# Stick-breaking attention in a hybrid block: the scan's zero operand in PSUM, 513-wide scans from two sigmoid tiles, two query buffers

## The chip, the cores and the metric

The kernel runs on one core of a Trainium2 chip. TensorE (PE) multiplies into PSUM, VectorE (DVE), ScalarE (ACT) and GpSimd (POOL) do the elementwise work, and SyncE (SP) issues the DMAs. The metric is the device time of one execution in microseconds.

## The reference

One layer over 2048 tokens of 1024 features: a modulated norm, one input projection, two groups of heads, an output projection with residual, a second modulated norm, and a convolutional feed-forward part. The change lies in the stick-breaking attention of eight heads of 64:

```python
def stick_breaking_attention(q, k, v):
    """A[t,s] = beta_ts * prod_{s<j<t}(1-beta_tj), s<t, in log space."""
    ...
        z = jnp.einsum('bhqd,bhkd->bhqk', qb, kb).astype(jnp.float32) * scale
        mask = s_pos[None, :] < t_pos[:, None]
        log_one_minus = jnp.where(mask, jax.nn.log_sigmoid(-z), 0.0)
        shifted = jnp.concatenate(
            [log_one_minus[..., 1:], jnp.zeros_like(log_one_minus[..., :1])], axis=-1)
        between = lax.cumsum(shifted, axis=3, reverse=True)
        weights = jnp.where(mask, jnp.exp(jax.nn.log_sigmoid(z) + between), 0.0)
        outs.append(jnp.einsum('bhqk,bhkd->bhqd', weights.astype(vb.dtype), vb))
```

Per query the weight of a key is its sigmoid times the product of (1 - sigmoid) over all later keys, so a running product from the last key back to the first is wanted.

## The kernel before

The program has three parts: the input projection with the gated linear attention (to about 663 us in the profile), the stick-breaking attention with the output projection running alongside (to about 1400 us), and the feed-forward part. The attention works on units (j, h, ci): 512 queries of chunk j, head h, 512 keys of chunk ci, from ci = j (the diagonal one) down to 0. Four chunks and eight heads give 80 units; each has four steps of 128 queries, so there are 320 steps n: 32 in the first chunk of queries, 64, 96 and 128 in the following ones. Half of the second chunk's steps, a third of the third's and a quarter of the fourth's are diagonal ones, which are 128, 256, 384 and 512 keys wide; all others are 512 wide.

Step n issues in this order: `score(n)`, two products of queries (high and low parts) and keys into a PSUM tile z of two buffers, and on the diagonal a product with a mask; `weigh(n-1)`; `turned(n-6)`, the transposes of the weights into a PSUM tile tr; `value(n-8)`, two products with the values into av. In `weigh`, ACT writes om = sigmoid(-z/8) and bt = sigmoid(z/8); DVE scans om in place from the last column to the first (a running product: multiply by the element, add zero), and POOL multiplies bt by om shifted by one column. Column 512 of om holds what the running product was at the end of the next later keys' unit: a copy of column 0 of the om of four steps before, which is also the scan's start value. In `turned`, ACT copies tr to ah and DVE subtracts, al = tr - ah. PE's order in the loop is that of the program (`in_order`); the order on the other engines is set by a planner that simulates the program.

PSUM has eight banks. In the first chunk of queries they hold z (2), tr (2), av (2) and the sums of the last input projection; `swap_pools` then gives tr a third bank (`t2`, every third turn) and the output projection one. `project` puts the output projection of chunk j among the steps of chunk j+1 as 64 groups of three products, at a rate that spreads them over the chunk; after the first chunk it starts 24 steps late. `fetch` loads, six steps ahead, keys (kt), values (vt) and, for a new head, queries (qh, ql; pool `qp`, three buffers). In the fourth chunk POOL also makes sums for the feed-forward part (`early_sums`, tiles tq).

Of the kernel before, what the change touches and what calls it, by code (L numbers as in the profile page):

```python
# [16 lines left out]
P = 128  # L17
# [3 lines left out]
CH = 512  # L21
# [26 lines left out]
def hybrid_block(ctx, tc, x, c, w_ada, b_ada, g1, w_in, w_fg2, b_fg2, g_gla, w_out, g2,  # L48
# [24 lines left out]
    def in_order(engines=None):  # L73
        """what the block traces is issued, on each engine, in the order of the program"""
# [57 lines left out]
    # ================= in-projection and gated linear attention =================  # L132
# [15 lines left out]
    # small parameters, rows of 128 turned into columns  # L148
# [20 lines left out]
    def ada_sum(m, acc):  # L169
        """products of silu(c) and the rows of w_ada, still to be summed over the partitions"""  # L170
# [14 lines left out]
    def column_sums(acc):  # L185
        """the sums over the partitions of 1024 columns, as columns"""
        tp = ps_tp.tile([P, CH], F, name="tp")
        for k in range(KD):
            pe.matmul(out=tp[:, k:k + 1], lhsT=acc[:, k * P:(k + 1) * P], rhs=ones[:, 0:1], start=True, stop=True)
        return tp[:, :KD]  # L190

    # scale and shift before the in-projection, as columns
# [4 lines left out]
    def ada_load(ks, buf, off, cuts):  # L197
        """the columns of w_ada for the shift and scale of some of the features"""
# [8 lines left out]
    def ada_columns(ks, w, name):  # L207
        """their products with silu(c), as columns"""
# [37 lines left out]
    # columns of the convolution's parameters  # L246
# [10 lines left out]
    # strict suffix sums within chunks of 64, and the chunks' indicators  # L257
# [32 lines left out]
    def w_block(c0):  # L290
        """128 columns: [k][hi, lo] as (128 rows, 128 columns)"""
# [7 lines left out]
    def w_rows(c0, n):  # L299
        """n columns, all rows: [k][hi, lo]"""  # L300
# [14 lines left out]
    def load_gla(k0, n, pl, s=None):  # L315
        """rows of the weights of GLA's queries and keys"""
# [6 lines left out]
    def split_gla(k0, n, s, w=None, lo=None):  # L323
        """their parts, with the forget gate's first product behind the keys: by k, [hi, lo]"""
# [12 lines left out]
    def gla_parts(ws):  # L337
        """the weights of 128 queries, again, and of the keys and the forget gate: [k][hi, lo]"""
# [7 lines left out]
    def norm_x(j, tt):  # L346
        """128 rows of x over their norm"""
# [16 lines left out]
    def turn_x(j, k):  # L364
        """128 of the features for the whole chunk: turned, modulated, and split"""
# [39 lines left out]
    # A tile of 128 tokens (two chunks of the recurrence) is laid out with a head's parity and a token of a chunk on the  # L405
    # partitions, and with the chunk, the pair of heads and the features along them; queries and keys are zero outside of
    # their own head, so that a product over a pair of heads has no columns to spare.
# [12 lines left out]
    def gla_tile(ti):  # L420
        """a tile of 128 tokens, in stages"""
# [54 lines left out]
    def by_parity(t_):  # L476
        """columns (pair of heads, head, n) taken as (head, pair of heads, n)"""
        return t_.rearrange("p (a b n) -> p b a n", a=2, b=2)
# [26 lines left out]
    def gla_inputs(j, wq, wk, begun=None):  # L505
        """GLA's queries, keys and log decays of a chunk; the sums may have been made"""
# [22 lines left out]
        # log of the forget gate (times 16): min(z, 0) - ln(1 + exp(-|z|))  # L529
# [19 lines left out]
        # the chunks' whole decays  # L549
# [11 lines left out]
    def gla_rows(j, w, gated):  # L561
        """GLA's values, or its output gate, of a chunk"""
# [12 lines left out]
    def heads_qk(j, w, b):  # L575
        """128 of the attention's queries (b < 4) or keys of a chunk"""
# [36 lines left out]
    # The forget gate's second product in one pass: its rows are the low parts and the bias's, then from row 32 on the high  # L613
    # parts (for the high and low parts of what they multiply) and the bias's.
# [18 lines left out]
    def plan(half):  # L633
        """per piece: what loads its weights, its products for a chunk, whether a GLA tile goes with it"""
# [987 lines left out]
```

## Time and profile before

| | |
|---|---|
| median of 3 runs | 2779.56 us (2771.99 to 2781.61) |
| profiled execution, span from the first to the last instruction | 2785.1 us |
| PE busy over the span | 92% |
| DVE, ACT, POOL busy | 71%, 47%, 46% |
| attention's scans (DVE, 320) | 437.1 us, 1366 ns each |
| their copies of one column (DVE, 192) | 26.5 us, 138 ns each |
| POOL's multiplies of the attention (320) | 323.7 us, 1013 ns each |

The profile gives no other time for its execution than the span. The shares are averages over parts with different limits: the engine that is full differs between the parts, so the attention has to be read by its stretches. Busy time of an engine is the time from an instruction's start to its end, whatever it does in it.

### The profile page before, as it was taken

How to read it: one execution, taken by the hardware profiler on the slowest of the kernel's cores; microseconds unless marked ns; L12 is line 12 of the kernel's file. 1: busy time of each engine (PE TensorE's matmuls, PEld its weight loads, DVE VectorE, ACT ScalarE, POOL GpSimd, SP SyncE). 2: the span in 40 equal slices, each digit the busy share in tenths (PEclk: the TensorE clock that was granted, in tenths of full speed). 3: DMA queues.
4: the chain of work that ended last, by engine and by line, in shares of the span. 5: the costliest groups of instructions: out<-in, count | busy, mean ns of one | idle time of the engine just before them, and what ended most of it. 6: DMA issues, size and time to landing. Idle time of an engine off the chain costs nothing. (4 is left out here: it accounts for less than half of the span.)

```text
span 2785.1 us, 36760 instructions
## 1 busy us (share of the span) xinstructions
PE 2556.8 (92%) x12118; PEld 2073.0 (74%) x12118; DVE 1973.2 (71%) x2826; ACT 1299.9 (47%) x2316; POOL 1267.6 (46%) x1044
## 2 busy tenths in 40 slices
PE   6999999999798888888899999998999999999996
PEld 5788788888576666666677777776777777888885
DVE  6435551346989999999876767678778787454668
ACT  4423243324756666666554444445444444333343
POOL 2202131122444444766464554657656653262446
PEclk9999999999999999999999999999999999999998
DMA  8568854586854443444282433345544455544472
GB/s 282 178 189 260 251 172 144 177 240 187 260 152 141 118 123 112 139 135 125 76 255 97 136 117 113 122 158 179 166 140 154 148 164 202 191 149 141 155 265 80
DMA packets 406831, 459.10 MB, mean 165 GB/s; under 512 B 35806, under 2 KB 271596, under 8 KB 404592
## 3 DMA queue, kind: packets, MB, share of 16 engines
q1 hardware_dynamic: 406640, 456.74, 52.1%
q8 instruction: 96, 1.57, 0.2%
q14 instruction: 95, 0.78, 0.1%
HBM read 313.51 MB, written 143.13 MB: 164 GB/s over the span
## 5 line engine op out<-in xcount | busy, mean ns | idle before, releaser
L992 POOL TENSOR_TENSOR bt<-bt,om 128x512 f32<-128x512 f32 (+2 forms) x320 | 323.7, 1013 | 346.4 <-DVE om L991 201.2
L991 DVE TENSOR_TENSOR_SCAN om<-om,zeros 128x512 f32<-128x512 f32 (+2 forms) x320 | 437.1, 1366 | 23.0 <-ACT om L979 22.3
L1169 POOL TENSOR_TENSOR wub<-ring,wub 128x512 fp32r<-128x512 f32 x176 | 233.6, 1338 | 269.6 <-ACT wub L1168 268.6
L979 ACT ACTIVATE om<-z 128x512 f32<-128x512 f32 (+2 forms) x320 | 171.8, 537 | 204.9 <-PE z L967 83.9
L1215 PE MATMUL v<-h,wua 128*128 128x512 f32 x1056 | 259.4, 394 | 7.6 <-DVE eh L901 3.9
L1215 PE MATMUL v<-h,wub 128*128 128x512 f32 x1056 | 251.7, 395 | 13.4 <-DVE v L1219 13.4
L1215 PE MATMUL g<-h,wub 128*128 128x512 f32 x1056 | 257.6, 390 | 0.0
L1215 PEld LDWEIGHTS v<-h,wub 128*128 128x128 f32 x1056 | 201.0, 191 | 57.4 <-issue 8.3
L1169 POOL TENSOR_TENSOR wua<-ring,wua 128x512 fp32r<-128x512 f32 x132 | 197.8, 1501 | 95.9 <-ACT wua L1168 93.7
L1164 DVE TENSOR_TENSOR ring<-ring 128x512 f32<-128x512 f32 x176 | 180.1, 1043 | 86.0 <-DMA ring<-in_w_up_dram 71.0
L1215 PEld LDWEIGHTS v<-h,wua 128*128 128x128 f32 x1056 | 198.4, 189 | 55.2 <-ACT wub L1168 5.6
L1215 PEld LDWEIGHTS g<-h,wub 128*128 128x128 f32 x1056 | 198.2, 188 | 41.8
L1588 PE MATMUL d<-h,wub 128*128 128x512 f32 x924 | 222.9, 391 | 0.0
L70 PE MATMUL tr<-ident,bt 128*128 128x128 f32 x1120 | 181.5, 279 | 35.7 <-DVE al L130 25.2
L1346 POOL TENSOR_TENSOR h<-h,h 128x512 fp32r<-128x512 f32 x77 | 116.9, 1521 | 191.0 <-ACT h L1345 187.2
L1588 PEld LDWEIGHTS d<-h,wub 128*128 128x128 f32 x924 | 173.5, 188 | 37.6
L286 POOL TENSOR_TENSOR wr<-wst,wr 128x1024 fp32r<-128x1024 f32 x28 | 69.3, 2480 | 278.1 <-ACT wr L285 278.1
L130 DVE TENSOR_TENSOR al<-tr,ah 128x512 fp32r<-128x512 f32 (+1 forms) x320 | 192.6, 602 | 3.0 <-ACT ah L129 2.6
L1018 PE MATMUL av<-al,vt 128*128 128x512 f32 (+1 forms) x320 | 132.6, 414 | 65.6 <-DVE al L130 26.8
L129 ACT ACTIVATE ah<-tr 128x512 fp32r<-128x512 f32 (+1 forms) x320 | 177.6, 555 | 22.4 <-PE tr L70 21.5
L70 PEld LDWEIGHTS tr<-ident,bt 128*128 128x128 f32 x1120 | 133.0, 143 | 71.5 <-DVE al L130 20.0
L1168 ACT ACTIVATE wub<-ring 128x512 fp32r<-128x512 f32 x176 | 108.2, 626 | 141.0 <-DVE ring L1164 92.7
(302 smaller groups left out, 6042.3 us busy)
## 6 DMA issues: line engine op xcount, KB each, us to landing
ring<-in_w_up_dram SPq DMA_DIRECT2D x176, 256.0 KB, 4.0
ring<-hid_s SPq DMA_DIRECT2D x154, 256.0 KB, 4.3
wst<-in_w_in_dram SPq DMA_DIRECT2D x45, 512.0 KB, 8.0
hid_s<-cval SPq DMA_DIRECT2D x88, 256.0 KB, 2.2
kt<-k_hl SPq DMA_DIRECT2D x80, 256.0 KB, 3.0
vt<-v_hl SPq DMA_DIRECT2D x80, 256.0 KB, 3.3
hid_s<-ring SPq DMA_DIRECT2D x66, 256.0 KB, 2.3
ast<-in_w_ada_dram SPq DMA_DIRECT2D x32, 512.0 KB, 6.0
```

Source lines behind the costliest of these rows:

```text
L70: pe.transpose(out=o, in_=i, identity=ident)
L129: act.activation(out=hi, in_=ps, func=AF.Copy)
L130: dve.tensor_tensor(out=lo, in0=ps, in1=f32(hi), op=ALU.subtract)
L979: act.activation(out=om[:, :w], in_=z[:, :w], func=AF.Sigmoid, scale=-0.125)
L991: dve.tensor_tensor_scan(out=rev, data0=rev, data1=zeros[:, 0:1].broadcast_to([P, w]), initial=first, op0=ALU.mult, op1=ALU.add)
L992: pool.tensor_tensor(out=b1, in0=b1, in1=om[:, 1:w + 1], op=ALU.mult)
L1018: pe.matmul(out=av[:, vs], lhsT=vts[u][:, s], rhs=al[:, vs], start=False, stop=last)
L1164: dve.tensor_tensor(out=t_, in0=a, in1=b, op=op)
L1169: eng.tensor_tensor(out=t_[:, 1], in0=src, in1=f32(t_[:, 0]), op=ALU.subtract)
L1215: pe.matmul(out=ps, lhsT=lhsT, rhs=rhs, start=begin and k == 0 and m == 0, stop=k == KH - 1 and m == 2, skip_group_check=not begin)
L1346: pin(eng.tensor_tensor(out=t_[:, 1], in0=src, in1=f32(t_[:, 0]), op=ALU.subtract))
L1588: pin(pe.matmul(out=ps, lhsT=hd[:, l_, tsl], rhs=w[:, r_], start=begin and q == 0 and m == 0, stop=q == NQ2 - 1 and m == 2, skip_group_che ...
```

## The change

After the first chunk of queries the scan reads its zeros from a column in a PSUM bank of its own (`zero`), no longer from SBUF (`zeros`). That bank is taken from tr, which keeps two. Off the diagonal ACT writes its sigmoid to one of two tiles `sg` in turn, whose column 512 holds a constant one, and the scan goes over 513 columns from `sg` into om; column 512 of om thereby becomes the start value, and the copy of one column is gone. On the diagonal the scan stays in place. The query pool has two buffers. What else differs is comments.

```diff
     def swap_pools():
         fps.close()
-        pools["t2"] = psp(aps, "ps_t2", 1)
+        z0 = psp(aps, "ps_zero", 1).tile([P, 1], F, name="zero")
+        dve.memset(z0, 0.0)
+        zero[0] = z0
         pools["o"] = psp(aps, "ps_o", 1)
 
     def turn_tile():
         turns[0] += 1
-        return pools["t2" if "t2" in pools and turns[0] % 3 == 0 else "t"].tile([P, CH], F, name="tr")
+        return pools["t"].tile([P, CH], F, name="tr")
...
-    qp = sb(st, "qp", 3, "right")
+    qp = sb(st, "qp", 2, "right")
...
+    zero = [zeros]
+
+    sgs = [aone.tile([P, CH + 1], F, name=f"sg{i}") for i in range(2)]
+    for t_ in sgs:
+        pool.memset(t_[:, CH:], 1.0)
...
         om = omp.tile([P, CH + 1], F, name="om")
-        act.activation(out=om[:, :w], in_=z[:, :w], func=AF.Sigmoid, scale=-0.125)
+        if diag:
+            beta, first, n_ = om, 1.0, w
+        else:
+            beta, first, n_ = sgs[n % len(sgs)], oms[n - 4][:, 0:1], CH + 1
+        act.activation(out=beta[:, :w], in_=z[:, :w], func=AF.Sigmoid, scale=-0.125)
         act.activation(out=b1, in_=z[:, :w], func=AF.Sigmoid, scale=0.125)
         if diag:
             dve.memset(om[:, w:w + 1], 1.0)
             if r == 2:
                 pool.memset(bts[u][:, 2, w:], 0.0)
-            first = 1.0
-        else:
-            before = oms[n - 4]
-            dve.tensor_copy(out=om[:, CH:CH + 1], in_=before[:, 0:1])
-            first = before[:, 0:1]
-        rev = om[:, 0:w][:, ::-1]
-        dve.tensor_tensor_scan(out=rev, data0=rev, data1=zeros[:, 0:1].broadcast_to([P, w]), initial=first, op0=ALU.mult, op1=ALU.add)
+        dve.tensor_tensor_scan(out=om[:, 0:n_][:, ::-1], data0=beta[:, 0:n_][:, ::-1],
+                               data1=zero[0][:, 0:1].broadcast_to([P, n_]), initial=first, op0=ALU.mult, op1=ALU.add)
```

The planner keeps PE's order in the loop and moves little on the other engines. On DVE, in the off-diagonal steps of a head of the second chunk, the order before was this; a scan is listed as SCALAR_TENSOR_TENSOR, xt is the output projection's residual, eh a turned piece of the second norm:

```order
L867 TENSOR_TENSOR xt<-o,xt 128x512
L988 COPY om<-om 128x1
L991 SCALAR_TENSOR_TENSOR om<-om,zeros 128x512
L130 TENSOR_TENSOR al<-tr,ah 128x512
L988 COPY om<-om 128x1
L991 SCALAR_TENSOR_TENSOR om<-om,zeros 128x512
L130 TENSOR_TENSOR al<-tr,ah 128x512
L988 COPY om<-om 128x1
L901 TENSOR_SCALAR eh<-tr,ab_140 128x128 x4
L991 SCALAR_TENSOR_TENSOR om<-om,zeros 128x512
```

The first scan in it is the diagonal one of 512 columns; a copy stands ahead of each off-diagonal scan, sometimes by more than one instruction. After the change DVE has, in the same place:

```order
L869 TENSOR_TENSOR xt<-o,xt 128x512
L996 SCALAR_TENSOR_TENSOR om<-om,zero 128x512
L130 TENSOR_TENSOR al<-tr,ah 128x512
L996 SCALAR_TENSOR_TENSOR om<-sg_5196,om,zero 128x513
L130 TENSOR_TENSOR al<-tr,ah 128x512
L996 SCALAR_TENSOR_TENSOR om<-sg_5197,om,zero 128x513
L130 TENSOR_TENSOR al<-tr,ah 128x512
```

Scan and subtraction alternate with nothing between them. On PE the order differs only behind the last scores of the attention, where the output projection of the last chunk (into o, and into z, which is free by then) runs between the last turns. Before:

```order
L70 MATMUL tr<-ident,bt 128x128 x4
L862 MATMUL z<-wo_5813,mgh 128x512
L863 MATMUL z<-wo_5813,mgh 128x512
L864 MATMUL z<-wo_5813,mgl 128x512
...
L862 MATMUL z<-wo_6241,mgh 128x512
L1017 MATMUL av<-ah,vt 128x512
L863 MATMUL z<-wo_6241,mgh 128x512
L864 MATMUL z<-wo_6241,mgl 128x512
L1018 MATMUL av<-al,vt 128x512
L70 MATMUL tr<-ident,bt 128x128 x4
```

After it, PE has in the same place:

```order
L864 MATMUL z<-wo_5817,mgh 128x512
L865 MATMUL z<-wo_5817,mgh 128x512
L866 MATMUL z<-wo_5817,mgl 128x512
...
L864 MATMUL z<-wo_6526,sh_12062 128x512
L865 MATMUL z<-wo_6526,sh_12062 128x512
L70 MATMUL tr<-ident,bt 128x128 x4
L1023 MATMUL av<-ah,vt 128x512
L1024 MATMUL av<-al,vt 128x512
```

Seventeen products of the projection stand together there, ahead of a turn that stood ahead of the first of them. On SP the query loads move: in the second chunk a head's four pieces lie together, where they were spread over several loads before.

## Rows read from the trace of the kernel before

**Rows 1.** Stretches of the attention: busy time per engine, granted clock, DMA share.
```profile
core 0: us, PE busy (x) PEld busy (x) DVE busy (x) ACT busy (x) POOL busy (x), PEclk, DMA share, GB/s
663.00:715.00 52.00, 46.00 (x286) 36.94 (x285) 48.44 (x102) 40.81 (x105) 27.58 (x39) 1.00 0.71 226
715.00:780.00 65.00, 49.08 (x262) 36.20 (x261) 64.45 (x105) 46.90 (x104) 30.05 (x37) 0.95 0.79 235
780.00:864.00 84.00, 83.79 (x460) 68.72 (x458) 69.43 (x137) 51.46 (x113) 34.21 (x41) 1.00 0.52 151
864.00:1086.00 222.00, 189.54 (x1001) 146.04 (x1001) 218.05 (x363) 149.83 (x313) 101.26 (x110) 0.98 0.42 121
1086.00:1379.00 293.00, 237.25 (x1223) 179.90 (x1222) 284.51 (x433) 193.61 (x394) 186.44 (x168) 0.98 0.39 116
1379.00:1440.00 61.00, 60.67 (x293) 50.10 (x291) 39.67 (x74) 26.91 (x47) 29.12 (x24) 1.00 0.76 247
```

**Rows 2.** DVE groups, 715 to 780: busy us, mean ns, idle before.
```profile
L991 DVE TENSOR_TENSOR_SCAN om<-om,zeros 128x512 f32<-128x512 f32 x20 | 34.1, 1707 | 0.0
```

**Rows 3.** DVE groups, 780 to 864.
```profile
L991 DVE TENSOR_TENSOR_SCAN om<-om,zeros 128x512 f32<-128x512 f32 x20 | 25.9, 1297 | 8.3 <-ACT om L979 8.2
```

**Rows 4.** PE groups, 780 to 864: output projection, one of three each.
```profile
L862 PE MATMUL o<-wo,sh 128*128 128x512 f32 x32 | 12.7, 396 | 0.0
...
L862 PE MATMUL o<-wo,mgh 128*128 128x512 f32 x28 | 11.1, 396 | 0.0
```

**Rows 5.** DVE groups, 864 to 1086.
```profile
L991 DVE TENSOR_TENSOR_SCAN om<-om,zeros 128x512 f32<-128x512 f32 x72 | 114.0, 1584 | 0.9 <-ACT om L979 0.9
...
L988 DVE COPY om<-om 128x1 f32<-128x1 f32 x64 | 8.8, 138 | 0.5
L991 DVE TENSOR_TENSOR_SCAN om<-om,zeros 128x128 f32<-128x128 f32 x8 | 7.3, 908 | 0.0
```

**Rows 6.** DVE groups, 1086 to 1379.
```profile
L991 DVE TENSOR_TENSOR_SCAN om<-om,zeros 128x512 f32<-128x512 f32 x104 | 170.1, 1635 | 1.6 <-ACT om L979 1.5
...
L988 DVE COPY om<-om 128x1 f32<-128x1 f32 x96 | 13.2, 137 | 2.1 <-POOL bt L992 0.3
...
L991 DVE TENSOR_TENSOR_SCAN om<-om,zeros 128x128 f32<-128x128 f32 x7 | 7.3, 1038 | 0.0
```

**Rows 7.** Order of time, DVE and POOL near 785: start, duration, engine.
```profile
785.18 1.23 DVE L991 TENSOR_TENSOR_SCAN om<-om,zeros 128x512 f32<-128x512 f32 x1 [0.48 <-ACT om L979]
...
786.55 1.09 POOL L992 TENSOR_TENSOR bt<-bt,om 128x512 f32<-128x512 f32 x1 [2.20 <-DVE om L991]
```

**Rows 8.** Order of time, DVE and POOL near 1204.
```profile
1203.84 0.66 DVE L130 TENSOR_TENSOR al<-tr,ah 128x512 fp32r<-128x512 f32 x1
...
1204.42 1.09 POOL L992 TENSOR_TENSOR bt<-bt,om 128x512 f32<-128x512 f32 x1
1204.42 0.14 DVE L988 COPY om<-om 128x1 f32<-128x1 f32 x1
1204.48 2.10 DVE L991 TENSOR_TENSOR_SCAN om<-om,zeros 128x512 f32<-128x512 f32 x1
...
1205.46 1.65 POOL L1055 TENSOR_TENSOR tq<-tq,tq 128x256 f32<-128x256 f32 x1
```

**Rows 9.** Single lines over the whole trace: shortest, median, longest in ns.
```profile
L991 DVE TENSOR_TENSOR_SCAN om<-om,zeros x320: 403/1290/2172, 662.7 to 1376.5; 128x512 f32<-128x512 f32 x96, 128x128 f32<-128x128 f32 x32, 128x384 f32<-128x384 f32 x32
...
L130 DVE TENSOR_TENSOR al<-tr,ah x320: 388/659/692, 671.3 to 1389.2; 128x512 fp32r<-128x512 f32 x128, 128x256 fp32r<-128x256 f32 x32
...
L1271 DVE SCALAR_TENSOR_TENSOR cval<-v,conv_w,cval x44: 1275/1283/1285, 1466.1 to 2334.2; 128x1023 f32<-128x1023 f32 x44
```

**Rows 10.** Order of time, two of four PE products in a row.
```profile
782.34 0.39 PE L862 MATMUL o<-wo,sh 128*128 128x512 f32 x1
...
783.04 0.40 PE L862 MATMUL o<-wo,sh 128*128 128x512 f32 x1
```

**Rows 11.** DVE groups, whole trace: a subtraction within SBUF.
```profile
L1164 DVE TENSOR_TENSOR ring<-cval,ring 128x512 f32<-128x512 f32 x22 | 15.1, 684 | 0.0
```

**Rows 12.** Query loads over the whole trace, from issue to landing.
```profile
DMA to landing us min/median/max: 2.4/3.5/12.9
```

## The prediction

> **What bounds the kernel now.** I read the stretches first, then within each the VectorE (DVE) groups, then single instructions in order of time. Only the attention is touched, from 663 to about 1379 us. Its first chunk of queries ends near 715 us, the second near 864, the third near 1086, the fourth near 1379. In [rows 1] DVE is busy 64.45 of 65 us in the first half of the second chunk, 218.05 of 222 in the third, 284.51 of 293 in the fourth. There TensorE (PE) stands at 49 of 65, 190 of 222 and 237 of 293, ACT at 150 of 222 and 194 of 293. Only from 780 to 864 us, where the out-projection of the first chunk is pressed into half a chunk, is PE the full one (83.79 of 84) and DVE at 69.43. So DVE ends last in three stretches, PE in one, and PE again behind the attention (60.67 of 61 in the last row).
>
> What fills DVE is the scan. A 512-wide scan took 1.23 us where POOL's multiply began only after it [rows 7]. Its mean is 1.707, 1.584 and 1.635 us in the three DVE-bound stretches [rows 2, 5, 6], and 1.297 in the PE-bound one [rows 3]. In [rows 8] the reason is seen: POOL's multiply runs from 1204.42 for 1.09 us, a scan that began at 1204.48 shows 2.10 us, and POOL's next instruction, begun at 1205.46 in the scan's time, shows 1.65 us and ends only after it. Scan and multiply take turns: what the profile calls busy DVE is partly waiting for POOL. Two kinds of DVE instruction never stretch in this way [rows 9]: the subtraction al<-tr,ah (one operand in PSUM, one in SBUF) stays between 388 and 692 ns over all widths and 320 instances, and the multiply-add cval<-v,conv_w,cval (a PSUM operand, an SBUF operand and a column scalar in SBUF) between 1275 and 1285 ns. The changed scan has the shape of the second: sigmoids in SBUF, zeros in PSUM, a start value from an SBUF column.
>
> In the Trainium skill, page "SBUF — State Buffer", section "Who interferes with whom", a DVE instruction with two SBUF inputs contends with a GpSimd instruction that reads SBUF, and one with at most one SBUF input does not. Rows 8 and 9 agree.
>
> **The change part by part.**
>
> Zeros in PSUM. I take 1.27 us for a scan from then on: between 1.23 alone and the 1.297 of the PE-bound stretch. The 513th column is one part in 512, nothing at this resolution. Freed DVE time, 512-wide: 20 x (1.707-1.27) = 8.7 us before 780; 72 x (1.584-1.27) = 22.6 in the third chunk; 104 x (1.635-1.27) = 38.0 in the fourth. The 128-wide scans took 0.908 and 1.038 us on average there [rows 5, 6], against a smallest scan of all of 0.403 [rows 9]; with 0.42 for them that is 8 x 0.49 = 3.9 and 7 x 0.62 = 4.3. The 256- and 384-wide ones I leave at about 1 us a chunk. The three earliest wide scans and the first chunk's are issued before the zero column in PSUM exists, and gain nothing.
>
> No row has a scan that reads PSUM. Nearest below: scan alone, 1.23. For a surcharge of the operand's place the nearest rows are al<-tr,ah at 512 columns, which [rows 8] shows at 0.66, and the same operation with both operands in SBUF and no stretch, 0.684 [rows 11]: none. I take none. At the far end stands a scan that is slowed per column; that is a rival below.
>
> The Trainium skill, page "VectorE: DVE Perf Modes", section "The TRN2 errata", gives DVE a fixed cost of 58 cycles with SBUF sources and 120 with a PSUM source at 0.96 GHz. By it each scan would lose 65 ns, and the freed time over 196 scans would be about 13 us less. Rows 8 and 11 show no such difference for the subtraction.
>
> No single-column copies. 192 fall away, 64 in the third chunk and 96 in the fourth, at 0.138 us [rows 5, 6]. But the next scan starts 0.06 us after the copy's start (1204.42 to 1204.48, [rows 8]), so only that is freed: 1, 3.8 and 5.8 us.
>
> Freed in sum: 9.7 us before 780, 31 in the third chunk, 50 in the fourth; 91 in all. In 780 to 864 nothing is freed that counts, since PE ends it.
>
> What is late next. PE's products follow each other 0.23 us apart when nothing waits (782.34 to 783.04 for three, [rows 10]). The stretch 780 to 864 has 3 x 32 + 3 x 28 = 180 out-projection products [rows 4], 41.4 us, which leaves 42.6 us for its 32 steps, 1.33 a step. The third chunk then needs 96 x 1.33 + 192 x 0.23 = 172 us of PE, the fourth 128 x 1.33 + 44 = 214; at the granted 0.98 of [rows 1] 175 and 219. DVE would need 218-31 = 187 and 284.5-50 = 234.5. PE is then at 94% of DVE, ACT at 80%. Before, DVE idled 1 to 3% with PE at about 80% of it. With the next engine so close I allow 6%: 54.8/0.94 = 58.3 for 65 us, 187/0.94 = 199 for 222, 234.5/0.94 = 249.5 for 293, gains of 6.7, 23 and 43.5: **73 us**. With 3% idle it would be 89, with 12% 39. These are the ends of this term.
>
> The two sigmoid tiles are a new wait: ACT's sigmoid of step n waits for the scan of step n-2, and ACT's later sigmoid and the copies ah queue behind it, for which DVE's al and then PE's av wait. Cover: the tile comes free at the end of scan n-2, and DVE then has al (0.66) and scan n-1 (1.27) and another al to do, 2.6 us, while ACT needs 0.6 for the sigmoid. Nothing on the path while ACT runs within one step of DVE; it has 20% to spare. The order on ACT hardly moves.
>
> Two turning banks for three: the transposes of step n wait for al two turns earlier. In PE's order the product of that same al stands right behind those transposes, so the wait existed and moves ahead by one group of transposes. Where a normalized tile is turned, a bank is held longer, by four tensor_scalars; that is inside the 6%.
>
> Two query buffers. This matters for the first chunk, whose heads take 52/8 = 6.5 us: a head's queries are then loaded after the last scores of the head two before, about one head ahead. Landing took 3.5 us in the median, 12.9 at most [rows 12]. So 0, and up to 13 us if two of the six loads land like the slowest. I take 0.
>
> Behind the attention PE's order changes as shown: 17 products of the last out-projection stand in a row ahead of the last four turns (17 x 0.23 = 3.9 us). PE is full there, so I take 0 +/- 3. The feed-forward part starts when this ends, and moves with it.
>
> Sum: -73. The span was 2785.1 us, 5.5 above the median of the runs; I take the difference off both: span about 2712, median 2779.6-73 = **2706**.
>
> **The rivals.**
>
> Rings bind. The two tiles, two banks and two z banks let DVE run dry whenever PE or ACT is late. For: PE comes to 94% of DVE. Against: each ring's loop, worked above, leaves over 1 us a step. At 12% idle the gain is 39, the time 2741.
>
> It doesn't do what it says. The scan still takes turns with POOL, because of its SBUF start column or its output. Then only the copies are gained, 11 us, some of it lost in the rings: about 2770. Against: the multiply-add in [rows 9] has such a column and such an output and is steady.
>
> Slower, by one mechanism: the scan streams its second operand more slowly from PSUM. Between 0.403 and 1.23 us from 128 to 512 columns it takes 2.15 ns a column. With half as much again it would be 1.23 + 512 x 1.08/1000 = 1.78 us: 20 x 0.07 + 72 x 0.20 + 104 x 0.145 = 31 us more, less 11 of the copies, 2800. It decides from about 1.67 us on (the stretched mean plus the copy's 0.06). Against: the subtraction from PSUM keeps its pace.
>
> **How the numbers follow.** The forecast 0.78; rings bind 0.13; no effect 0.04; slower scan 0.05. A change of 0.3%, 8.3 us, is about what a measurement can tell from none; the rival at 2770 lies on that border, so half of it counts as same. Faster 0.93, same 0.02, slower 0.05. The forecast's own range is 2690 (3% idle) to about 2730; the range wanted takes in the rings at 2741 and a late query load beyond: 2686 to 2744. The slower and the idle rival stay out.
>
> **What would show it.** In the profile after, the wide scans should be near 1.25 us with a spread of some hundredths, POOL's multiplies near 1.09 without instances of 2; no copies; the third chunk some 199 and the fourth some 250 us long; 780 to 864 and the feed-forward part unchanged in length; DVE still the fullest engine of the attention, PE close. Scans above 1.67 us, or still up to 2.1, would prove me wrong at the root; ACT waiting for om<-sg, or PE's tr for al, more than 10% of a chunk would show the rings.

## The result and the profile after

The changed kernel takes **2712.92 us** (median, 2709.53 to 2718.57) against 2779.41 for the kernel before on the same chip: a ratio of 0.9762, 95% interval 0.9744 to 0.978, or 66.5 us less. The prediction was 2706 us in a range of 2686 to 2744. The profiled execution has a span of 2716.8 us against 2785.1.

The last scan of the attention begins at 1293.4 us, where it was 1376.5 [rows 9]. So 83 us are gained inside the attention, and only 68 of them are left at the end of the span. Two things have to be explained: why the attention gained more than the 73 us forecast, and where 15 us went behind it.

The costliest groups of the whole trace of the changed kernel that belong to the attention (busy us, mean ns | idle us before them):

```profile
L998 POOL TENSOR_TENSOR bt<-bt,om 128x512 f32<-128x512 f32 (+2 forms) x320 | 311.9, 977 | 289.8 <-DVE om L996 176.9
...
L996 DVE TENSOR_TENSOR_SCAN om<-sg,om,zero 128x513 f32<-128x513 f32 x189 | 239.8, 1269 | 11.5 <-ACT sg L990 11.1
```

Single lines of the changed kernel over the whole trace, shortest, median and longest in ns; they answer to [rows 9]:

```profile
L996 DVE TENSOR_TENSOR_SCAN om<-sg,om,zero x189: 1259/1267/1284, 728.7 to 1293.4; 128x513 f32<-128x513 f32 x189
...
L996 DVE TENSOR_TENSOR_SCAN om<-sg,om,zeros x3: 1355/2077/2086, 722.2 to 726.1; 128x513 f32<-128x513 f32 x3
...
L998 POOL TENSOR_TENSOR bt<-bt,om x320: 407/1092/1540, 663.7 to 1294.8; 128x512 f32<-128x512 f32 x96, 128x128 f32<-128x128 f32 x32, 128x384 f32<-128x384 f32 x32
```

Of 189 scans with zeros in PSUM the shortest and the longest are 25 ns apart. The three that were issued before the PSUM column existed still stretch, up to 2086 ns, in the same program and the same stretch. That is the change's mechanism within a single trace.

Order of time near 1132 us in the changed kernel (start, duration, engine), the same place in a step as [rows 8]:

```profile
1132.29 1.26 DVE L996 TENSOR_TENSOR_SCAN om<-sg,om,zero 128x513 f32<-128x513 f32 x1
1132.65 1.09 POOL L998 TENSOR_TENSOR bt<-bt,om 128x512 f32<-128x512 f32 x1
...
1133.48 0.66 DVE L130 TENSOR_TENSOR al<-tr,ah 128x512 fp32r<-128x512 f32 x1
1133.70 0.74 POOL L1061 TENSOR_TENSOR tq<-tq,tq 128x256 f32<-128x256 f32 x1
1134.06 1.26 DVE L996 TENSOR_TENSOR_SCAN om<-sg,om,zero 128x513 f32<-128x513 f32 x1
```

POOL's multiply lies wholly inside a scan and neither is any longer for it: 1.26 and 1.09 us, where [rows 8] had 2.10 for the scan. POOL's tq takes 0.74 us, where it had 1.65 beside a scan.

The stretches of the attention, cut at the starts of the same scans in both kernels (the first and the middle one of the second chunk, the first of the third and of the fourth, the last of all). [rows 1] cuts the third chunk's end some 5 us behind the fourth chunk's first scan, so the kernel before stands here again, ahead of the changed one:

```profile
core 0: us, PE busy (x) PEld busy (x) DVE busy (x) ACT busy (x) POOL busy (x), PEclk, DMA share, GB/s
715.20:779.90 64.70, 48.78 (x261) 35.90 (x260) 64.19 (x104) 46.60 (x104) 29.79 (x36) 0.95 0.79 235
779.90:862.50 82.60, 82.39 (x451) 67.80 (x449) 68.03 (x135) 50.06 (x110) 33.73 (x40) 1.00 0.51 147
862.50:1080.90 218.40, 186.08 (x991) 143.32 (x989) 214.82 (x358) 147.94 (x310) 99.55 (x109) 0.98 0.41 119
1080.90:1376.50 295.60, 239.71 (x1230) 181.61 (x1231) 286.74 (x438) 196.84 (x401) 187.45 (x171) 0.97 0.40 119
```

```profile
715.40:770.60 55.20, 43.35 (x250) 31.66 (x249) 54.95 (x86) 46.36 (x102) 30.05 (x36) 1.00 0.89 261
770.60:854.30 83.70, 83.30 (x459) 68.98 (x458) 66.15 (x120) 50.16 (x109) 32.65 (x40) 1.00 0.49 152
854.30:1049.00 194.70, 176.74 (x988) 141.76 (x986) 184.53 (x295) 147.94 (x311) 98.28 (x109) 0.98 0.45 134
1049.00:1293.40 244.40, 223.43 (x1229) 174.00 (x1230) 235.38 (x343) 193.76 (x400) 153.29 (x171) 0.99 0.49 147
```

DVE is busy 9.2, 30.3 and 51.4 us less in the three stretches that it bounded, 90.9 in all. They are 9.5, 23.7 and 51.2 us shorter; the one that PE bounds is longer by 1.1. DVE is still the fullest engine of the three, with PE right behind (177 and 223 us in the third and fourth chunk).

DVE groups of the changed kernel, 1049 to 1295 us (they answer to [rows 6]):

```profile
L996 DVE TENSOR_TENSOR_SCAN om<-sg,om,zero 128x513 f32<-128x513 f32 x96 | 121.6, 1267 | 2.2 <-ACT sg L990 2.0
...
L996 DVE TENSOR_TENSOR_SCAN om<-om,zero 128x512 f32<-128x512 f32 x8 | 9.7, 1218 | 1.9 <-ACT om L990 1.8
...
L996 DVE TENSOR_TENSOR_SCAN om<-om,zero 128x128 f32<-128x128 f32 x8 | 3.2, 404 | 0.0
```

### The profile page after: what moved, and what is told of

The parts are those of the page before. It is cut to its first block, busy times and chain, and to the rows that moved or that the text cites. A ratio compares the mean times of both kernels' runs of the same rounds, so it can differ in the third digit from the quotient of the medians.

```text
span 2716.8 us, 36444 instructions
## 1 busy us (share of the span) xinstructions
PE 2534.6 (93%) x12118; PEld 2066.8 (76%) x12118; DVE 1872.4 (69%) x2635; ACT 1298.6 (48%) x2316; POOL 1229.2 (45%) x1046
## 5 line engine op out<-in xcount | busy, mean ns | idle before, releaser
L998 POOL TENSOR_TENSOR bt<-bt,om 128x512 f32<-128x512 f32 (+2 forms) x320 | 311.9, 977 | 289.8 <-DVE om L996 176.9
L996 DVE TENSOR_TENSOR_SCAN om<-sg,om,zero 128x513 f32<-128x513 f32 x189 | 239.8, 1269 | 11.5 <-ACT sg L990 11.1
L1170 DVE TENSOR_TENSOR ring<-ring 128x512 f32<-128x512 f32 x176 | 173.5, 1006 | 94.5 <-DMA ring<-in_w_up_dram 79.9
L70 PEld LDWEIGHTS tr<-ident,bt 128*128 128x128 f32 x1120 | 126.7, 142 | 107.6 <-DVE al L130 52.9
L400 PE MATMUL mm<-wr,hh 128*128 128x512 f32 (+1 forms) x448 | 170.0, 379 | 3.5 <-DVE vt L130 2.0
L991 ACT ACTIVATE bt<-z 128x512 f32<-128x512 f32 (+2 forms) x320 | 172.1, 538 | 0.0
```

Of the source, the lines that this page charges most:

```text
L70: pe.transpose(out=o, in_=i, identity=ident)
L400: pe.matmul(out=ps[:, :n], lhsT=hh[:, k, sl], rhs=wh, start=k == 0, stop=False)
L991: act.activation(out=b1, in_=z[:, :w], func=AF.Sigmoid, scale=0.125)
L996: dve.tensor_tensor_scan(out=om[:, 0:n_][:, ::-1], data0=beta[:, 0:n_][:, ::-1], data1=zero[0][:, 0:1].broadcast_to([P, n_]), initial=firs ...
L998: pool.tensor_tensor(out=b1, in0=b1, in1=om[:, 1:w + 1], op=ALU.mult)
L1170: dve.tensor_tensor(out=t_, in0=a, in1=b, op=op)
```

## The experiments

Four lengths are read from each profile. "Attention" runs from the start of the first scan to that of the last one; "tail" from there to the first product of the feed-forward part (v); "first step" from that to the first gate; "gates" from the first to the last of the 44 gates, which is the up-projection. A gate is counted from ACT's Silu of it. Ratios are against the kernel before, run beside it on the same chip. Every length is that of one profiled execution.

| kernel | median us | ratio, 95% | attention | tail | first step | gates |
|---|---|---|---|---|---|---|
| before | 2779 to 2782 | 1 | 713.8 | 53.2 | 43.4 | 868.3 |
| changed kernel | 2712.92 | 0.9762 (0.9744 to 0.978) | 630.3 | 58.0 | 46.5 | 875.7 |
| e0_after_again | 2714.02 | 0.9754 (0.9728 to 0.9781) | 630.5 | 58.0 | 45.9 | 874.1 |
| f0_after_third | 2711.24 | 0.9758 (0.9742 to 0.9774) | 627.6 | 56.9 | 44.8 | 871.5 |
| e4_tr_two | 2792.61 | 1.004 (1.0025 to 1.0056) | 717.6 | 57.3 | 45.8 | 870.0 |
| e1_zero_only | 2722.21 | 0.9791 (0.9765 to 0.9817) | 642.4 | 58.6 | 45.6 | 866.3 |
| e2_sg_only | 2778.39 | 0.9992 (0.9978 to 1.0007) | 709.6 | 53.2 | 45.3 | 867.8 |
| e3_qp_two | 2784.73 | 1.0018 (1.0003 to 1.0032) | 712.2 | 53.2 | 44.0 | 874.9 |
| e5_no_multiply | 2694.34 | 0.9695 (0.9676 to 0.9715) | 620.1 | 53.7 | 44.8 | 867.2 |
| e7_memset_pool | 2706.13 | 0.9752 (0.9728 to 0.9776) | 627.7 | 56.9 | 45.1 | 867.7 |
| f7_memset_pool_again | 2709.97 | 0.9751 (0.973 to 0.9772) | 627.6 | 56.9 | 46.3 | 865.0 |
| e8_memset_eh | 2720.91 | 0.9788 (0.9773 to 0.9803) | 633.2 | 58.9 | 52.8 | 869.8 |
| f1a | 2708.28 | 0.9746 (0.9729 to 0.9763) | 630.0 | 59.1 | 45.6 | 868.9 |
| f1b | 2710.24 | 0.9751 (0.9735 to 0.9766) | 629.9 | 55.9 | 44.3 | 867.3 |

The changed kernel itself was run twice more (e0_after_again and f0_after_third), as the measure for the others.

> The changed kernel once more, as a second execution to tell what repeats. My theory: the attention's last scan ends near 1295 us (before: 1378), 84 us earlier, and some 5 us are lost between it and the feed-forward part's first product (51.2 us before, 56.6 in the first profile), which repeats, since the order of instructions is fixed. The further 10 us that the first profile lost inside the feed-forward part are partly jitter: I expect 3 to 10 us there. Rival: all 15 us repeat to within 2 us. Time 2713 +/- 4.

> The changed kernel a third time, as the base for the three others of this call. Theory: the attention 630 us from the first scan's start to the last one's, the stretch from there to the feed-forward part's first product 58 us, both within 1 us of the two earlier profiles; the feed-forward part's first 44 gates between 866 and 876 us. Time 2713 +/- 4.

The times hold, and in both the tail is again longer than before, by 4.8 and 3.7 us. First step and gates together are 8.3 us longer than before in e0_after_again, within the 3 to 10 expected, and 4.6 in f0_after_third. But f0_after_third has an attention 2.7 us shorter than the first profile's and a tail 1.1 us shorter, where 1 us was the bound: a difference of 3 us between two profiles says little.

**The change taken apart.** First the lost bank alone: the kernel before with two turning banks.

```diff
-        pools["t2"] = psp(aps, "ps_t2", 1)
...
-        return pools["t2" if "t2" in pools and turns[0] % 3 == 0 else "t"].tile([P, CH], F, name="tr")
+        return pools["t"].tile([P, CH], F, name="tr")
```

> The kernel before with two tr banks instead of three and nothing in the eighth bank. Theory: in the attention the missing bank costs little, 0 to 4 us, because DVE sets the pace; behind it PE's order is the changed kernel's (17 products of the projection in a row), and 5 us are lost from the last scan to the feed-forward part's first product (56 instead of 51). In all 2782 to 2788, ratio 1.001 to 1.003. Rival (two banks make the transposes wait): slower by 20 us or more, all of it inside the attention. Rival for the loss behind the attention (it comes from the earlier end, when weights and sums aren't there yet): 51 us here as before.

It costs 11 us, more than expected. In the one profile of each, 3.8 us of it lie in the attention, little more than two profiles of one kernel differ by, and 4.1 in the tail; the rest lies in the first step and the gates. The wide scans stretch as before, 1576 ns on average where [rows 2, 3, 5, 6] make 1593 over their 216 (DVE group over the attention, e4_tr_two):

```profile
L990 DVE TENSOR_TENSOR_SCAN om<-om,zeros 128x512 f32<-128x512 f32 x216 | 340.5, 1576 | 13.9 <-ACT om L978 13.5
```

Then the zeros in that bank, with the copies, the scans in place and three query buffers left as they were.

```diff
-        pools["t2"] = psp(aps, "ps_t2", 1)
+        z0 = psp(aps, "ps_zero", 1).tile([P, 1], F, name="zero")
+        dve.memset(z0, 0.0)
+        zero[0] = z0
...
-        return pools["t2" if "t2" in pools and turns[0] % 3 == 0 else "t"].tile([P, CH], F, name="tr")
+        return pools["t"].tile([P, CH], F, name="tr")
...
-        dve.tensor_tensor_scan(out=rev, data0=rev, data1=zeros[:, 0:1].broadcast_to([P, w]), initial=first, op0=ALU.mult, op1=ALU.add)
+        dve.tensor_tensor_scan(out=rev, data0=rev, data1=zero[0][:, 0:1].broadcast_to([P, w]), initial=first, op0=ALU.mult, op1=ALU.add)
```

> The kernel before with the zeros read from PSUM and, for its bank, two tr banks; copies, 512-wide scans in place and three query buffers stay. Theory (the scan no longer takes turns with POOL): scans of 512 near 1.25 us instead of 1.6, the copies cost 0.06 us each, so the gain is 66 less 8 to 10: 2720 to 2726, ratio 0.979 to 0.981. Rival (the gain is from the 513-wide scan out of place or from the missing copies): close to 2770, ratio 0.995 or more.

2722.2 us, as expected; against e4_tr_two, measured beside it, that is 70.4 us less, 75.2 in the attention. DVE groups of e1_zero_only, 715 to 1400 us:

```profile
L994 DVE TENSOR_TENSOR_SCAN om<-om,zero 128x512 f32<-128x512 f32 x212 | 267.9, 1264 | 15.9 <-ACT om L982 15.2
...
L991 DVE COPY om<-om 128x1 f32<-128x1 f32 x192 | 27.0, 141 | 3.1
...
L994 DVE TENSOR_TENSOR_SCAN om<-om,zeros 128x512 f32<-128x512 f32 x4 | 6.8, 1712 | 0.0
```

The wide scan falls from 1576 to 1264 ns on average with nothing but its second operand moved. With 212 of them that is 66 us of the 75.

Third, the sigmoid tiles without the zeros in PSUM: the changed kernel, with its scans reading `zeros` in SBUF and the third turning bank back.

```diff
-        z0 = psp(aps, "ps_zero", 1).tile([P, 1], F, name="zero")
-        dve.memset(z0, 0.0)
-        zero[0] = z0
+        pools["t2"] = psp(aps, "ps_t2", 1)
...
-        return pools["t"].tile([P, CH], F, name="tr")
+        return pools["t2" if "t2" in pools and turns[0] % 3 == 0 else "t"].tile([P, CH], F, name="tr")
```

> The changed kernel with the zeros back in SBUF and the third tr bank back: 513-wide scans from two sigmoid tiles, no copies, two query buffers. Theory: the scans still take turns with POOL, mean near 1.6 us; only the copies' 0.06 us are gained: 2766 to 2772, ratio 0.995 to 0.997. Rival (the copies and the out-of-place scan carry the gain): 2725 or less, scans near 1.27 us.

A miss: 2778.4 us, not to be told from the kernel before. 192 copies are gone, and the attention is only 4.2 us shorter, hardly more than two profiles of one kernel differ by. DVE groups of e2_sg_only from 715 to 1400 us (513 wide off the diagonal, 512 wide on it), and the line's first group from shortest to longest over the trace:

```profile
L994 DVE TENSOR_TENSOR_SCAN om<-sg,om,zeros 128x513 f32<-128x513 f32 x192 | 317.6, 1654 | 11.1 <-ACT sg L988 10.7 <-POOL bt L996 0.2
L994 DVE TENSOR_TENSOR_SCAN om<-om,zeros 128x512 f32<-128x512 f32 x25 | 35.4, 1417 | 5.1 <-ACT om L988 5.1
```

```profile
L994 DVE TENSOR_TENSOR_SCAN om<-sg,om,zeros x192: 1265/1809/2169, 726.8 to 1377.4; 128x513 f32<-128x513 f32 x192
```

The wide scans together take 353.0 us for 217, where they took 344.1 for 216 [rows 2, 3, 5, 6]: less one scan of 1.6 us that is 7 us more. Of the 192 x 0.06 = 11.5 us that the copies took from DVE, 7 are then eaten by longer scans, which leaves the 4 that the attention gained. A scan that starts 0.06 us earlier, beside the same multiply of POOL, mostly ends no earlier: it waits longer. That reading fits [rows 8], where copy and multiply begin together; no run shows it directly. The same edit on top of the zeros in PSUM is another matter: from e1_zero_only to the changed kernel measured beside it (2722.2 to 2714.0) it gains 8.2 us, and 12 in the attention (642.4 to 630.5); that step also takes the third query buffer. The intervals of the two ratios overlap, so the 8.2 are not clear of the noise; the attention of the changed kernel, at 627.6 to 630.5 in three profiles, is shorter by 12 to 15. So it seems that the whole of the copies could be saved only once scan and multiply no longer took turns.

Last, the query buffers alone.

```diff
-    qp = sb(st, "qp", 3, "right")
+    qp = sb(st, "qp", 2, "right")
```

> The kernel before with two query buffers instead of three, nothing else. Theory: no cost, since a head's queries are issued about one head ahead: within 3 us of before, ratio 0.999 to 1.001, the first chunk's eight heads (663 to 715 us) not longer than 53 us. Rival: the first chunk waits for its queries, 5 us or more there.

The time is 5.3 us above the kernel before, beyond the 3 us expected, by an interval that nearly reaches no change. The attention, the only place where these buffers are used, is no longer than before (712.2 against 713.8; its first chunk takes 52.4 us from first scan to first scan in both), nor the tail; what its profile has more lies in the gates, whose order of instructions is the same. The buffers cost nothing that these runs can show.

In sum: the bank +11, the zeros -70.4, the sigmoid tiles with the buffers -8.2: -67.6 from 2781.6 to 2714.0.

**The suspected cause taken away by itself.** If scan and multiply take turns, then without the multiply the scan must be short with its zeros still in SBUF. This kernel is the one before, less one line:

```diff
-        pool.tensor_tensor(out=b1, in0=b1, in1=om[:, 1:w + 1], op=ALU.mult)
```

> The kernel before without POOL's multiply of the attention: the weights stay without their product over later keys. All scans stay in place with zeros in SBUF, copies and three tr banks stay. Theory (the scan is stretched by waiting for POOL's multiply): 512-wide scans near 1.23 us with hardly any above 1.3, the attention 60 to 85 us shorter than before (714 us from the first scan's start to the last one's), time near 2710 to 2720. Rival (the scan is slow because of its two operands in SBUF, whatever POOL does): scans stay near 1.6 us and the attention within 10 us of before.

DVE group of e5_no_multiply, 715 to 1330 us, and the line from shortest to longest:

```profile
L991 DVE TENSOR_TENSOR_SCAN om<-om,zeros 128x512 f32<-128x512 f32 x215 | 274.6, 1277 | 12.8 <-ACT om L979 12.3
```

```profile
L991 DVE TENSOR_TENSOR_SCAN om<-om,zeros x320: 401/1268/1725, 659.0 to 1279.1; 128x512 f32<-128x512 f32 x96, 128x128 f32<-128x128 f32 x32, 128x384 f32<-128x384 f32 x32
```

The scan is at 1277 ns with both operands in SBUF; POOL's other work is still there, and a few scans of up to 1725 ns with it. The scan's own pace was never the trouble, POOL's multiply beside it was. The attention is 93.7 us shorter than before and the time 2694.3, both beyond what was expected (60 to 85, and 2710 to 2720): besides the shorter scans, nothing behind the multiply waits for it any more. At 620.1 us the attention is only 10 less than in the changed kernel, though this kernel also has its third turning bank, so little can be left of what this contention cost.

**What bounds the attention now.** DVE still looks full. Two edits take work off it. The first, the memset of the diagonal's last column on POOL:

```diff
-            dve.memset(om[:, w:w + 1], 1.0)
+            pool.memset(om[:, w:w + 1], 1.0)
```

> The changed kernel with the constant one behind the diagonal scans written by POOL instead of DVE. Theory: DVE still ends last in the first half of the second chunk and in the third and fourth (99%, 95% and 96% busy), and loses 80 instructions of 0.06 us there: 2 to 5 us faster than the changed kernel, near 2710. Rival: PE, at 91% of these stretches, ends last as often as DVE, and nothing is gained (2713 +/- 2).

> The constant ones behind the diagonal scans by POOL, again, beside the changed kernel on one chip. Theory: the attention is 2 to 4 us shorter (627.7 in the first profile against 630.4), the rest is that of the changed kernel, so 2 to 5 us faster: ratio to before 0.0007 to 0.0018 lower than that of the changed kernel. Rival: the earlier 7 us between their medians were wholly the feed-forward part's scatter, and the two agree within 2 us.

2706.1 and 2710.0 us. The second is 1.3 us less than f0_after_third, measured beside it, and by their ratios (0.9752 and 0.9751, where the changed kernel has 0.9754 to 0.9762) no gain is shown. The attention of 627.6 and 627.7 us that was to show the gain is that of f0_after_third too. The second edit adds half of the second norm's scaling on ACT:

```diff
-                dve.tensor_scalar(out=eh[:, sl], in0=held[g][:, sl], scalar1=ab2[:, 1, k:k + 1],
-                                  scalar2=ab2[:, 0, k:k + 1], op0=ALU.mult, op1=ALU.add)
+                if i % 2:
+                    act.activation(out=eh[:, sl], in_=held[g][:, sl], func=AF.Identity, scale=ab2[:, 1, k:k + 1],
+                                   bias=ab2[:, 0, k:k + 1])
+                else:
+                    dve.tensor_scalar(out=eh[:, sl], in0=held[g][:, sl], scalar1=ab2[:, 1, k:k + 1],
+                                      scalar2=ab2[:, 0, k:k + 1], op0=ALU.mult, op1=ALU.add)
```

> The kernel with POOL's constant ones, and half of the scaling of the turned second norm (eh, 128 instructions of 0.4 us on DVE) given to ACT. Theory (DVE ends last): another 3 to 8 us, near 2704. Rival (PE ends last by now, 177 of 195 us in the third chunk): no difference from the constant ones alone.

Stretches of e7_memset_pool, then of e8_memset_eh (columns as above):

```profile
854.00:1049.00 195.00, 176.93 (x995) 142.11 (x996) 184.94 (x261) 148.08 (x310) 99.75 (x142) 0.99 0.45 135
1049.00:1292.00 243.00, 222.79 (x1228) 173.27 (x1228) 232.91 (x310) 190.77 (x393) 153.62 (x196) 1.00 0.47 143
```

```profile
854.00:1049.00 195.00, 175.85 (x982) 140.05 (x982) 179.03 (x241) 154.58 (x328) 99.29 (x140) 0.99 0.45 134
1049.00:1292.00 243.00, 221.28 (x1213) 172.96 (x1212) 228.71 (x291) 197.01 (x409) 152.33 (x195) 0.99 0.47 143
```

In the same windows DVE is busy 6 and 4 us less, and PE does not get further but a little less far (176 and 221 us of products, where it had 177 and 223). The time is 2720.9 us, 14.8 above e7_memset_pool measured beside it (the intervals of the two ratios just touch): neither the gain of the theory nor the tie of the rival. The attention is 5.5 us longer than in e7_memset_pool, the tail 2.0 and the first step 7.7; in that step PE waits 7.1 us for the turned norm's ht of DVE and 5.3 for an eh of ACT. Taking 10 us off the fullest engine, and putting 6 and 6 us on ACT for it, has lost time: after the change DVE, at 95 to 96%, is no longer what alone sets the pace. ACT's waits in e8_memset_eh, 854 to 1290 us (total, count, longest):

```profile
ACT sg L994 <- PE z L976: 38.4, 73, 2.0
```

ACT waits for PE's scores, and PE (in the changed kernel's waits, below) for al, which needs ACT's ah and DVE. The engines wait for each other around a loop, and which link of it would have to be shortened was not settled.

**The tail.** In the table the tail is 53.2 to 53.7 us in the four profiles with three turning banks (before, e2, e3, e5) and 55.9 to 59.1 in the ten with two. With two banks PE has 17 products of the last projection in a row, ahead of turns that stood ahead of them. To see whether that order is the cause, the last turns borrowed z banks, which are free by then; f1a is e7_memset_pool with this, f1b the same with `extra % 2 == 1`:

```diff
-        tr = turn_tile()
+        extra = n - (N - LEAD + 1)
+        tr = ps_z.tile([P, CH], F, name="z") if extra >= 0 and extra % 3 == 2 else turn_tile()
```

> As the constant ones by POOL, and every third turn behind the last scores uses one of the two z banks, which are free by then. Theory (the loss behind the attention comes from PE's order with two tr banks): turns and products alternate again, and the stretch from the last scan to the feed-forward part's first product falls from 57 to 53 or 54 us; time 3 us below the constant ones alone. Rival (it comes from the sums and weights not being there): it stays at 57.

> As the constant ones by POOL, and every second turn behind the last scores uses a z bank: the planner puts the last turns ahead of the projection, with few products between them. Theory: PE then waits for the last weights (up to 6 steps of about 1.9 us, less what lies between), and gains the turn of the last normalized tile earlier; between 53 and 60 us for that stretch, no better than every third turn. Rival: the earlier the turns, the shorter the stretch: 52 or less.

The tail is 59.1 us in f1a and 55.9 in f1b. Neither has the order of the kernel before: f1a still has runs of 21 and 22 products ahead of turns. f1b is within the 53 to 60 expected, but it is better than f1a, which it was not to be. In time the two are not to be told from e7_memset_pool (0.9746 and 0.9751).

What differs is PE's wait behind the attention's last products with values. The longest wait of the tail in the kernel before, the changed kernel, f1a, and the wait for the same in f1b (total, count, longest; sh is the high part of the attention's last sums, which ACT and DVE make from av and which the projection's last products read):

```profile
PE o L862 <- DVE xt L867: 0.3, 1, 0.3
PE o L864 <- ACT sh L1038: 2.3, 1, 2.3
PE o L864 <- ACT sh L1039: 2.1, 1, 2.1
PE o L864 <- ACT sh L1039: 0.3, 1, 0.3
```

Between the last product with values and the first one that needs sh, PE has 13 products of the projection in the four profiles with three banks, 8 in f1b and none in the nine others. Where there are none it stands still for 2.1 to 2.3 us there. So the order that comes with two banks does cost time: what would have covered the wait has been issued ahead of the last turns. f1a moved products and turns but left none to cover it. The tails of the kernel before, the changed kernel, f0_after_third and f1a (columns as above):

```profile
1376.50:1429.70 53.20, 52.87 (x258) 43.66 (x257) 34.36 (x66) 22.40 (x41) 21.84 (x19) 1.00 0.70 227
1293.40:1351.40 58.00, 55.71 (x265) 45.50 (x264) 33.01 (x64) 23.19 (x42) 22.24 (x19) 0.97 0.63 209
1287.10:1344.00 56.90, 54.29 (x265) 44.58 (x265) 32.08 (x64) 23.13 (x42) 22.36 (x19) 1.00 0.64 213
1287.80:1346.90 59.10, 56.10 (x266) 45.71 (x266) 33.85 (x64) 23.33 (x42) 22.32 (x19) 0.97 0.61 205
```

In f0_after_third, at the same granted clock as before, PE's products take 1.4 us more (7 more of them are left behind the last scan's start) and its waits 2.3 more, which makes the 3.7 of the tail. In the changed kernel's first profile and in f1a the granted clock is 0.97, and the products take 1.4 and 1.8 us more than in f0_after_third; so f1a's 59.1 against the 56.9 of e7_memset_pool is mostly the clock. In the first step, too, PE waits longer. The kernel before, then the changed one, behind the first product of the feed-forward part:

```profile
PE v L1215 <- DVE eh L901: 3.9, 1, 3.9
...
PE v L1215 <- DVE halo L1281: 1.3, 1, 1.3
```

```profile
PE v L1221 <- DVE eh L903: 5.8, 1, 5.8
...
PE v L1221 <- DVE halo L1287: 2.5, 1, 2.5
```

The last turned piece of the second norm (eh) comes later, and so does the halo of the first gate: 1.9 and 1.2 us, the 3.1 by which that step is longer in the first profile. In the repeats it is 2.5 and 1.4. Why eh is later was not settled. That the tail's 4 us go with the missing bank is shown, since e4_tr_two has them with no other edit, and the wait for sh with them (2.3 us).

## Why the prediction came out as it did

**The bound, and the scan: right.** 1.27 us was taken for the wide scan, 1.264 to 1.270 was measured (the 1.23 that stood as the lower bound was a diagonal scan, with a constant start, as the last section shows); 0.42 for the 128-wide one, 0.404 to 0.405. POOL's multiply was to be near 1.09 without instances of 2: the median is 1092 ns, the longest 1540. The freed DVE time was put at 91 us and is 90.9, stretch by stretch 9.2 for 9.7, 30.3 for 31 and 51.4 for 50. The bet that carried this, that a column start value in SBUF and an output in SBUF do not count while zeros in PSUM take the scan out of POOL's way, was made from the steady multiply-add of [rows 9], and holds for 189 scans. The Trainium skill's rule in "SBUF — State Buffer", "Who interferes with whom", agrees with it for the scan too.

**No surcharge for PSUM: right, and against a page.** The diagonal scans of 512 columns took 1.218 us with zeros in PSUM, where the diagonal scan of [rows 7], alone and with zeros in SBUF, took 1.23; the others, which start from a column, 1.264 to 1.270 against 1.27 for such a scan in e5_no_multiply, with zeros in SBUF (last section). The estimate of 65 ns a scan from the two fixed costs in the Trainium skill, page "VectorE: DVE Perf Modes", section "The TRN2 errata", does not show in these scans; the 13 us of that sum were rightly left out.

**No copies: right in size here, for a reason only half seen.** 0.06 us each, 10.6 in all, was taken; the step from e1_zero_only to the changed kernel shows 12 in the attention and 8.2 in time, the latter not clear of the noise. But the rival that the scan still takes turns with POOL priced the copies at 11 us on their own, about 2770 us, and e2_sg_only shows that alone they bring nothing measurable (4 us in the attention). The parts do not add independently: here most of a gain on an engine that waits for another went into the wait.

**What is late next: mis-sized.** The 6% idle that was allowed for the next engine, to turn 91 us freed into 73 gained, was too much in two stretches of three. DVE idles 0.5% (54.95 of 55.2), 5.2% (184.53 of 194.7) and 3.7% (235.38 of 244.4), so the three stretches gained 9.5, 23.7 and 51.2 us where 6.7, 23 and 43.5 were forecast: 84.4 us for 73. The third chunk came out as forecast, the fourth carries most of the difference. PE's times, forecast at 175 and 219, came to 177 and 223. The signal named for binding rings was ACT waiting for om<-sg, or PE's tr for al, beyond a tenth of a chunk. The changed kernel's waits, 1049 to 1295 us:

```profile
PEld tr L70 <- DVE al L130: 23.8, 33, 1.8
ACT sg L990 <- PE z L972: 21.7, 40, 1.9
PE tr L70 <- DVE al L130: 17.5, 21, 1.6
```

The wait of PE's weight loads (PEld) for al stands just below that mark (23.8 of 246 us), while ACT waits mostly for PE's z and not for a free sigmoid tile. Since al comes from an engine that is busy 96% there, the mark could not have told a ring that binds from a full DVE; it was badly chosen. The attention's share of the lost bank is 3.8 us by e4_tr_two, 0.5%, one profile against one.

**780 to 864 unchanged: right** (83.7 us for 82.6 from scan to scan). **Query buffers at 0: right**, as far as e3_qp_two can tell.

**The tail at 0 +/- 3, and a feed-forward part that only moves: wrong.** The first product of the feed-forward part in the kernel before (shortest, median, longest ns, then first and last start), and in the changed kernel:

```profile
L1215 PE MATMUL v<-h,wua x1056: 387/390/794, 1429.7 to 2322.9; 128*128 128x512 f32 x176
```

```profile
L1221 PE MATMUL v<-h,wua x1056: 387/390/764, 1351.4 to 2254.5; 128*128 128x512 f32 x176
```

It starts 78.3 us earlier, where the last scan starts 83.1 earlier. The tail is 4.8 us longer, and the step missed was the removed bank: it was weighed where DVE sets the pace, and behind the attention PE was taken as full whatever its order. With the order that two banks bring, PE waits 2.3 us for sh where it had 0.3. The first step is 3.1 us longer and the gates 7.4, though PE, DVE, ACT and POOL have the same instructions there, in the same order but for one on ACT and one on POOL that move by a place or two. Of the gates' 7.4 us, 4.9 are products that take longer: PE is busy there 829.28 us where it had 824.37, at a granted clock of 0.988 where it had 0.992. The clock differs in the same way between executions of one kernel: e7_memset_pool was granted 0.988 in its gates and f7_memset_pool_again 0.992, at 867.7 and 865.0 us. The gates vary between 865.0 and 875.7 us over all profiles; in the seven with 0.990 or more they take 865.0 to 868.9, in the seven below it 867.7 to 875.7. The changed kernel (871.5, 874.1 and 875.7) is at the long end of these, but so is e3_qp_two with 874.9. Whether the change causes any of it stays open.

So the mechanism and the freed time were right, and 2706 us was as near as it was partly by luck, from errors of opposite sign: 11 us too little gained in the three stretches, and 15 us given back behind the attention, with 1 in the stretch that PE bounds, that the sum did not have. The profiled executions then differ by 68.3 us, since the span of before lies 5.7 us above its median and that of after 3.9 us, which leaves the 66.5 us of the medians.

## What to carry to other kernels

When two engines' elementwise instructions stretch each other, look in the trace for an instruction of the same engine that keeps its time beside the same neighbour and compare where its operands lie: here moving one constant operand to PSUM was worth 70 us, and without that the removal of 192 instructions from the full engine was worth next to nothing. Price the resource that pays for it, a PSUM bank, over the whole stretch in which it is missing and not only where the gain is; where an engine's order changes with it, look for the wait that the old order covered. When the fullest engine is relieved, take the idle share of the next stretch from one in which two engines are already close (DVE at 97% with PE at 81% became 96% with PE at 91%), and treat work taken off at that point as unpriced until it has run: here moving 10 us of it to another engine made the kernel slower.

## What the runs showed of the hardware

A scan that starts from a column in SBUF takes about 0.05 us more than one with a constant start: 1.267 us against 1.218 in the same stretch of the changed kernel, both with zeros in PSUM. In e5_no_multiply, with zeros in SBUF, the two kinds stand likewise apart, as these two of DVE's scans in order of time show (the first one a diagonal step):

```profile
1068.26 1.23 DVE L991 TENSOR_TENSOR_SCAN om<-om,zeros 128x512 f32<-128x512 f32 x1 [0.25 <-ACT om L979]
...
1070.04 1.27 DVE L991 TENSOR_TENSOR_SCAN om<-om,zeros 128x512 f32<-128x512 f32 x1
```

A 513th column shows no cost that can be read. The 212 wide scans of e1_zero_only, all of 512 columns and 189 of them with a start column, take 267.9 us; in the changed kernel the 189 of 513 columns take 239.8 us and the 23 of 512, in this line, 28.0:

```profile
L996 DVE TENSOR_TENSOR_SCAN om<-om,zero 128x512 f32<-128x512 f32 x23 | 28.0, 1216 | 6.4 <-ACT om L990 6.1
```

Zeros in PSUM cost the scan nothing that shows: 1.218 us against 1.23 with a constant start, 1.267 against 1.27 with a start column. Its pace is about 2.1 ns a column (0.404 us for 128, 1.218 for 512: 0.814 us for 384 columns more).
